# Delta-rule stage of a two-block network: the filler projections leave PSUM by a ScalarE copy, and VectorE applies their row factor from SBUF

## The chip, the cores and the metric

The kernel runs on one core of a Trainium2 chip. The metric is device time in microseconds, lower is better: the median of three runs is 1378.98 us (1376.60 to 1381.67). The profile is of one further execution of 1386.14 us.

## What is computed

The input has 256 tokens of width 1024. A first block (token mixer and channel mixer) and a second block follow each other. The change lies in the middle of the second block, in its gated delta rule and multiscale pool:

```python
h = _rmsnorm(x, norm_mix_w[l])
proj = h @ w_in[l]
qkv = proj[..., :3 * DN_WIDTH]
z = proj[..., 3 * DN_WIDTH:4 * DN_WIDTH]
...
p = proj[..., 4 * DN_WIDTH + 2 * DN_HEADS:]
qkv = jax.nn.silu(_causal_conv(qkv, conv_w[l])).astype(jnp.float32)
q = _l2norm(qkv[..., :DN_WIDTH].reshape(b, s, DN_HEADS, DN_HEAD_DIM))
k = _l2norm(qkv[..., DN_WIDTH:2 * DN_WIDTH].reshape(b, s, DN_HEADS, DN_HEAD_DIM))
...
o = _chunk_gated_delta_rule(q, k, v, g, beta)
o = _rmsnorm(o, dn_norm_w[l]) * jax.nn.silu(z...)
pool_out = _multiscale_pool(p, w_pool[l], pool_scale[l]).astype(x.dtype)
x = x + jnp.concatenate([o, pool_out], axis=-1) @ w_out[l]
```

A lookup over 16384 experts (PEER) and a last norm follow. The delta rule holds a triangular inverse per head; the kernel builds it in blocks of 16 and then doubles the block size three times.

## The kernel before

Activations lie transposed: 128 channels on the partitions, 256 tokens along the free axis. A projection of 128 output channels is eight steps over the 1024 inputs, and each step is three matmuls (lines 375 to 377), because inputs and weights are split into a high and a low fp32r part. So a projection is 24 matmuls into one PSUM tile `pb`, of which there are three (`bufs=3`).

Weights come through a stream (class `Stream`): a DMA brings a `raw` tile of 512 KB (four of them), ScalarE rounds it to `whi` (line 218) and VectorE subtracts to get `wlo` (line 231). In this stage five such pairs exist, and a new DMA starts when a `wlo` has been made.

The rmsnorm's factor of each token, `rs` (tile `rbs`), is applied to a projection's result after the matmuls. So each projection ends with a step that reads PSUM, multiplies by `rs` and writes SBUF. That step also gives the PSUM tile back.

The stage has two strands. The main strand (`main`) is the delta rule: decay factors `dec` and the mask `N`, the products of k with k (line 1532), sums of squares and their reciprocal root (lines 1377, 425 to 448), the 16-block inverse as a long run of small VectorE instructions (lines 636 and 639, tiles `itmp` and `zd`), then its transpose `TT` and three doublings (lines 1581, 1591, 1586). The other strand (`filler`) holds the 16 projections for q, v, the pool p and z, in this order, and then the pool's half of the output projection. `weave` draws them against each other by weights written in the program, and a scheduler then fixes the order of each engine's instructions; each engine runs its own list strictly in that order.

A filler projection (`fproj`) runs 24 matmuls and hands its PSUM tile on; what follows it (multiply, convolution taps at line 1306, tanh, last product at line 1295, or the pool's windows at line 1424) is put into the list `post`, and one entry is taken from it at every matmul step of the following projections:

```python
for kt in range(KD):
    self.proj_step(ps, w, xs, kt)
    pop()
    yield 0.33
```

For q and v the first entry is `first` of `conv_ops` (line 1302, into tile `ct`), for the pool line 1434 (into `pp`), for z line 1415 (into `zt`). All are one VectorE `tensor_tensor` of 128 x 256 from PSUM. The four k projections come from before the stage and use `conv_ops` with a tile given from outside (`vn`).

Of the kernel before, what the change touches and what calls it, by code (L numbers as in the profile page):

```python
# [9 lines left out]
F32 = mybir.dt.float32  # L10
# [6 lines left out]
ALU = mybir.AluOpType  # L17
PSUM = bass.MemoryType.PSUM
P = 128
T = 256  # L20
# [276 lines left out]
class Builder:  # L297
# [949 lines left out]
    def delta(self, xs, pre, rs):  # L1247
        tc, nc, i, S = self.tc, self.nc, self.i, self.S
        x = self.x
        V, A, G = nc.vector, nc.scalar, nc.gpsimd  # L1250
        mm = nc.tensor.matmul
        b4 = lambda ps: ps.rearrange("p (c s) -> p c s", c=4)
        with tc.tile_pool(name="del", bufs=1) as dp:
# [7 lines left out]
            pp = t4("pp")  # L1261
# [7 lines left out]
            post = []  # L1269
# [7 lines left out]
            def fproj(eng):  # L1277
                ps = (self.pb if "f" in st else self.pa)()[:, 0:T]
                st["f"] = 1
                w = S.get()  # L1280
# [4 lines that stand above are left out]
                S.split(eng)  # L1285
                return ps

            def silu_ops(dst, src, th=None):
                d = {}

                def tanh():
                    d["th"] = dp.tile([P, T], F32, name="th", tag="th", bufs=4) if th is None else th
                    A.activation(d["th"], src, AF.Tanh, scale=0.5)

                return tanh, lambda: V.scalar_tensor_tensor(dst, d["th"], 1.0, src, ALU.add, ALU.mult)

            def conv_ops(dst, ps, ch, ct=None, th=None):
                d = {}

                def first():  # L1300
                    d["t"] = dp.tile([P, T], F32, name="ct", tag="ct", bufs=4) if ct is None else ct
                    V.tensor_tensor(d["t"], ps, rs, ALU.mult)  # L1302
                    A.activation(dst, d["t"], AF.Copy, scale=self.par("conv2", 36 + ch))

                def tap(s):
                    V.scalar_tensor_tensor(dst[:, s:T], d["t"][:, 0:T - s], self.par("conv2", (3 - s) * 12 + ch),
                                           dst[:, s:T], ALU.mult, ALU.add)

                tanh, last = silu_ops(dst, dst, th)
                return [first, lambda: tap(1), lambda: tap(2), lambda: (tap(3), tanh()), last]  # L1310

            sp = dp.tile([P, 2, 8], F32, name="sp")
            s24 = lambda n: dp.tile([P, 2, 4], F32, name=n)
# [44 lines left out]
            def head():  # L1358
                V.tensor_scalar(dnh, self.par("dn"), 0.5, None, ALU.mult)
                go = gate_ops()  # L1360
                next(go)
                vt = vn.rearrange("p (h a) t -> p h (a t)", h=4)
                kc = [conv_ops(k[:, h, :], ps, 4 + h, vt[:, h, :], o[:, h, :]) for h, ps in enumerate(pre)]
                for n in range(5):
                    for ops in kc:
                        ops[n]()
                        if n:
                            next(go, None)
                        yield YL[0]
                for _ in go:  # L1370
                    yield 0.2
# [29 lines left out]
            def conv_part(dst, base, name):  # L1401
                for h in range(4):
                    ps = yield from fproj(DS[h % 2])
                    c = conv_ops(dst[:, h, :], ps, base + h)
                    post.extend([c[0], None, c[1], c[2], c[3], None, c[4], None])
                post.append(lambda: st.update({name: 1}))

            def z_part():
                for h in range(4):
                    ps = yield from fproj(DZ[h % 2])  # L1410
                    t = dp.tile([P, T], F32, name="zt", tag="zt", bufs=2)
                    tanh, last = silu_ops(z[:, h, :], t)

                    def first(t=t, ps=ps, tanh=tanh):
                        V.tensor_tensor(t, ps, rs, ALU.mult)
                        tanh()

                    post.extend([first, None, None, last, None, None, None, None])

            def windows(g):  # L1420
                cur, s = pp[:, g, :], 1
                while s < win[g]:
                    n = dp.tile([P, T], F32, name="pw", tag="pw", bufs=3)
                    G.tensor_tensor(n[:, s:T], cur[:, s:T], cur[:, 0:T - s], ALU.add)
                    A.copy(n[:, 0:s], cur[:, 0:s])
                    cur, s = n, 2 * s
                st["p", g] = cur

            def pool_part():
                for g in range(4):  # L1430
                    ps = yield from fproj(DS[g % 2])

                    def first(g=g, ps=ps):
                        V.tensor_tensor(pp[:, g, :], ps, rs, ALU.mult)
                        windows(g)

                    def second(g=g):
                        cur = st["p", g]
                        V.tensor_tensor(cur[:, 0:16], cur[:, 0:16], self.con("rc", g * 16, g * 16 + 16), ALU.mult)
                        V.scalar_tensor_tensor(cur, cur, 1.0 / win[g], pp[:, g, :], ALU.mult, ALU.subtract)  # L1440

                    post.extend([first] + [None] * 6 + [second, lambda g=g: pool_mm(g)])
                post.append(lambda: st.update({"p": 1}))

            def filler():
                for part in ORD:
                    if part == "q":
                        yield from conv_part(q, 0, "q")
                    if part == "v":
                        yield from conv_part(v, 8, "v")  # L1450
                    if part == "z":
                        yield from z_part()
                    if part == "p":
                        yield from pool_part()
                while post:
                    pop()
                    yield 0.33
                while "acc" not in st:
                    yield 0.5
                for g in range(4):  # L1460
                    if g == NAR:
                        S.narrow()
                    yield from self.gout_step(st["acc"], (yah[:, g, :], yal[:, g, :]), g == 0, False)
                    S.split({"G": G, "V": V, "B": both}[GO[g]])

            def pool_mm(g):
                ps = self.pb()[:, 0:T]
                mm(ps, wpl[:, g * P:(g + 1) * P], st["p", g], start=True, stop=True)
                po = dp.tile([P, T], F32, name="po", tag="po", bufs=2)
                A.activation(po, ps, AF.Copy, scale=self.par("pool_scale", g))  # L1470
                self.split(yah[:, g, :], yal[:, g, :], po, G)
# [200 lines left out]
            for h in range(4):  # L1672
                ps = self.pb()
# [368 lines left out]
```

## Time and profile before

| | |
|---|---|
| median of three runs | 1378.98 us |
| profiled execution | 1386.14 us, of which the span is 1384.1 us |
| TensorE (PE) busy | 1341.7 us, 97% |
| VectorE (DVE) busy | 990.2 us, 72% |
| ScalarE (ACT) busy | 681.2 us, 49% |
| GpSimd (POOL) busy | 236.4 us, 17% |
| mean granted TensorE clock | 0.976 of full speed |

Times inside the profile are microseconds from the start of the span. PE is TensorE's matmuls, PEld its weight loads, SP the engine that issues DMAs. The delta-rule stage reaches from about 438 to 556 us. Names are the program's tiles without buffer numbers, L1302 is line 1302. A matmul's own duration overlaps with the next one's, so the pace is read from the distance between starts. [...]

### The profile page before, as it was taken

How to read it: one execution, taken by the hardware profiler on the slowest of the kernel's cores; microseconds unless marked ns; L12 is line 12 of the kernel's file. 1: busy time of each engine (PE TensorE's matmuls, PEld its weight loads, DVE VectorE, ACT ScalarE, POOL GpSimd, SP SyncE). 2: the span in 40 equal slices, each digit the busy share in tenths (PEclk: the TensorE clock that was granted, in tenths of full speed). 3: DMA queues.
4: the chain of work that ended last, by engine and by line, in shares of the span. 5: the costliest groups of instructions: out<-in, count | busy, mean ns of one | idle time of the engine just before them, and what ended most of it. 6: DMA issues, size and time to landing. Idle time of an engine off the chain costs nothing.

```text
span 1384.1 us, 26933 instructions
## 1 busy us (share of the span) xinstructions
PE 1341.7 (97%) x10572; PEld 1255.3 (91%) x10572; DVE 990.2 (72%) x2104; ACT 681.2 (49%) x1256; POOL 236.4 (17%) x218
## 2 busy tenths in 40 slices
PE   7989998999999799999999999999999999999998
PEld 6878997999998799999999999999998888888886
DVE  7863677888877886799995777888865555545554
ACT  3521355655565533465554554444444554554454
POOL 5610333010005240200000000000012222222221
PEclk9888998999999899999999999999999999999999
DMA  6140352566553132445555454544555555555553
GB/s 227 55 112 33 107 168 93 191 203 212 185 175 104 50 107 90 143 149 179 179 183 175 158 165 157 167 157 164 164 186 199 191 193 195 197 187 195 197 193 111
DMA packets 64334, 217.89 MB, mean 157 GB/s; under 512 B 10272, under 2 KB 11248, under 8 KB 64080
## 3 DMA queue, kind: packets, MB, share of 16 engines
q1 hardware_dynamic: 59376, 212.76, 46.5%
q0 software_dynamic: 992, 2.72, 0.7%
q8 instruction: 83, 1.36, 0.4%
q10 hardware_dynamic: 3840, 0.70, 0.4%
q14 instruction: 43, 0.35, 0.1%
HBM read 214.70 MB, written 1.44 MB: 156 GB/s over the span
## 4 chain that ended last, share of the span: by engine, by line
PE 87%; DVE 6%; ACT 2%; POOL 2%; DMA 1%; issue 1%; ACTq 0%; SPq 0%; POOLq 0%
PE pa L1950 25%; PE pb L375 15%; PE pb L376 15%; PE pb L377 15%; PE pa L375 3%; PE pa L376 3%; PE pa L377 3%; PE pc L1904 1%; PE pb L1904 1%; PE pa L1064 1%; PE pa L1581 1%; ACT whi L218 1%; DVE wlo L231 0%; PE pb L1838 0%; PE pc L463 0%
## 5 line engine op out<-in xcount | busy, mean ns | idle before, releaser
L218 ACT ACTIVATE whi<-raw 128x1024 fp32r<-128x1024 f32 x396 | 418.3, 1058 | 518.7 <-PE pb L376 260.4
L231 DVE TENSOR_TENSOR wlo<-raw,whi 128x1024 fp32r<-128x1024 f32 x382 | 467.1, 1223 | 249.8 <-ACT whi L218 248.7
L375 PE MATMUL pb<-xnh,whi 128*128 128x256 f32 x1024 | 294.3, 288 | 0.0
L376 PE MATMUL pb<-xnl,whi 128*128 128x256 f32 x1024 | 289.7, 283 | 0.0
L377 PE MATMUL pb<-xnh,wlo 128*128 128x256 f32 x1024 | 289.0, 283 | 0.0
L1950 PE MATMUL pa<-whi,up 128*128 128x512 f32 x1024 | 274.5, 389 | 0.0
L1950 PEld LDWEIGHTS pa<-whi,up 128*128 128x128 f32 x1024 | 192.2, 188 | 39.8
L376 PEld LDWEIGHTS pb<-xnl,whi 128*128 128x128 f32 x1024 | 196.1, 191 | 0.0
L375 PEld LDWEIGHTS pb<-xnh,whi 128*128 128x128 f32 x1024 | 195.9, 191 | 0.0
L377 PEld LDWEIGHTS pb<-xnh,wlo 128*128 128x128 f32 x1024 | 195.7, 191 | 0.0
L375 PE MATMUL pb<-xh,whi 128*128 128x256 f32 x648 | 187.8, 290 | 4.2 <-DVE ct L1302 4.2
L376 PE MATMUL pb<-xl,whi 128*128 128x256 f32 x648 | 185.6, 286 | 0.3
L377 PE MATMUL pb<-xh,wlo 128*128 128x256 f32 x648 | 185.4, 286 | 0.0
L1950 PE MATMUL pa<-wlo,up 128*128 128x512 f32 x512 | 158.3, 389 | 0.0
L503 POOL TENSOR_TENSOR up<-hb,up 128x256 fp32r<-128x256 f32 x32 | 45.9, 1434 | 553.3 <-ACT up L502 553.3
L375 PEld LDWEIGHTS pb<-xh,whi 128*128 128x128 f32 x648 | 123.7, 191 | 5.5 <-DVE ct L1302 4.4
L376 PEld LDWEIGHTS pb<-xl,whi 128*128 128x128 f32 x648 | 123.8, 191 | 1.5 <-DVE xl L569 0.9
L377 PEld LDWEIGHTS pb<-xh,wlo 128*128 128x128 f32 x648 | 123.7, 191 | 0.6
L1950 PEld LDWEIGHTS pa<-wlo,up 128*128 128x128 f32 x512 | 96.1, 188 | 20.0
L503 POOL TENSOR_TENSOR up<-scr,up 128x256 fp32r<-128x256 f32 x32 | 47.1, 1472 | 127.0 <-ACT up L502 127.0
L231 POOL TENSOR_TENSOR wlo<-raw,whi 128x1024 fp32r<-128x1024 f32 x19 | 46.5, 2453 | 43.3 <-ACT whi L218 34.4
L376 PE MATMUL pa<-al,whi 128*128 128x256 f32 x176 | 49.0, 281 | 0.0
(546 smaller groups left out, 2214.9 us busy)
## 6 DMA issues: line engine op xcount, KB each, us to landing
raw<-down SPq DMA_DIRECT2D x128, 512.0 KB, 3.3
raw<-up SPq DMA_DIRECT2D x128, 512.0 KB, 3.3
raw<-w_in SPq DMA_DIRECT2D x46, 512.0 KB, 3.4
raw<-w_up SPq DMA_DIRECT2D x44, 512.0 KB, 3.5
raw<-w_down SPq DMA_DIRECT2D x22, 512.0 KB, 3.4
raw<-w_out SPq DMA_DIRECT2D x16, 512.0 KB, 3.3
raw<-w_query SPq DMA_DIRECT2D x16, 512.0 KB, 3.4
x<-xT SPq DMA_DIRECT2D x4, 256.0 KB, 5.6
```

The source lines that it names most:

```text
L218: nc.scalar.activation(hi, self.raw[self.nh], AF.Copy)
L231: e.tensor_tensor(lo[:, a:z], raw[:, a:z], hi[:, a:z], ALU.subtract)
L375: mm(ps, w[0], x[0], start=start, stop=False, **k)
L376: mm(ps, w[0], x[1], start=False, stop=False, **k)
L377: mm(ps, w[1], x[0], start=False, stop=stop, **k)
L503: (eng or self.nc.vector).tensor_tensor(lo, src, hi.bitcast(F32), ALU.subtract)
L1064: mm(out[h, q], lh[h, 8 * hf + q, 0:64], self.halves(rh[h, 8 * hf + q, :], l, odd), start=True, stop=True)
L1581: mm(out[:, h], lh[:, tb * 4 + h, :], self.halves(rh[:, tb * 4 + h, :], l, odd), start=True, stop=True)
L1904: mm(ps[:, n, :], e1[:, q, :, r], eg[m][:, q, :, r], start=(m == 0), stop=(m == 1))
L1950: mm(acc[tb * 2 + hf], a[:, ts], b[:, hf * 512:hf * 512 + 512], start=False, stop=(e == 127 and lo == 1), skip_group_check=True)
```

## The change

Each of the 16 filler projections now leaves PSUM by a plain ScalarE copy, and VectorE multiplies by `rs` in place in SBUF. The copy is the first entry of `post`, the multiply the second. The k projections keep the old form.

```diff
             def conv_ops(dst, ps, ch, ct=None, th=None):
                 d = {}
 
+                def lift():
+                    d["t"] = dp.tile([P, T], F32, name="ct", tag="ct", bufs=4) if ct is None else ct
+                    A.copy(d["t"], ps)
+
                 def first():
-                    d["t"] = dp.tile([P, T], F32, name="ct", tag="ct", bufs=4) if ct is None else ct
-                    V.tensor_tensor(d["t"], ps, rs, ALU.mult)
+                    if "t" in d:
+                        V.tensor_tensor(d["t"], d["t"], rs, ALU.mult)
+                    else:
+                        d["t"] = ct
+                        V.tensor_tensor(ct, ps, rs, ALU.mult)
                     A.activation(dst, d["t"], AF.Copy, scale=self.par("conv2", 36 + ch))
...
-                return [first, lambda: tap(1), lambda: tap(2), lambda: (tap(3), tanh()), last]
+                return [first, lambda: tap(1), lambda: tap(2), lambda: (tap(3), tanh()), last, lift]
...
-                    post.extend([c[0], None, c[1], c[2], c[3], None, c[4], None])
+                    post.extend([c[5], c[0], c[1], c[2], c[3], None, c[4], None])
...
-                    def first(t=t, ps=ps, tanh=tanh):
-                        V.tensor_tensor(t, ps, rs, ALU.mult)
+                    def first(t=t, tanh=tanh):
+                        V.tensor_tensor(t, t, rs, ALU.mult)
                         tanh()
-                    post.extend([first, None, None, last, None, None, None, None])
+                    post.extend([lambda t=t, ps=ps: A.copy(t, ps), first, None, last, None, None, None, None])
...
-                    def first(g=g, ps=ps):
-                        V.tensor_tensor(pp[:, g, :], ps, rs, ALU.mult)
+                    def first(g=g):
+                        V.tensor_tensor(pp[:, g, :], pp[:, g, :], rs, ALU.mult)
                         windows(g)
...
-                    post.extend([first] + [None] * 6 + [second, lambda g=g: pool_mm(g)])
+                    post.extend([lambda g=g, ps=ps: A.copy(pp[:, g, :], ps), first] + [None] * 5 + [second, lambda g=g: pool_mm(g)])
```

The scheduler orders the instructions anew around this; the lists of all engines differ inside this stage alone. Three places show it. Lines behind the edit are numbered up to 7 higher in the changed kernel, and buffer numbers differ by a few. A line of "..." stands for rows left out, mostly the other matmuls of a projection.

TensorE before, around the main strand's way from k to the 16-block inverse: `pb_5930`, `pb_6104`, `pb_6200` and `pb_6240` are filler projections, `pa_5745` is k with k, `pc_5755` the sums of k's squares, `pa_5826` and `pa_5858` feed the 16-block inverse.

```order
L377 MATMUL pb_5930<-xh_5233,wlo_5570 128x256
L1532 MATMUL pa_5745<-k_5456 128x128 x4
...
L1377 MATMUL pc_5755<-ones_89,sq_5756 128x1 x2
...
L620 MATMUL pa_5826<-itmp_5776,con_del_3354 128x128
L629 MATMUL pa_5858<-dg_5774,sel_3362 128x128 x4
...
L375 MATMUL pb_6104<-xh_5233,whi_5639 128x256
...
L375 MATMUL pb_6200<-xh_5233,whi_5689 128x256
...
L375 MATMUL pb_6240<-xh_5233,whi_5838 128x256
```

Between k with k and the inverse no projection stands here.

The same place of TensorE in the changed kernel, where `pb_5934`, `pb_6109`, `pb_6206`, `pb_6247` are the same four projections, `pb_6288` and `pb_6401` the next two:

```order
L377 MATMUL pb_5934<-xh_5233,wlo_5570 128x256
L375 MATMUL pb_6109<-xh_5233,whi_5640 128x256
...
L1539 MATMUL pa_5748<-k_5456 128x128 x4
...
L375 MATMUL pb_6206<-xh_5233,whi_5691 128x256
...
L1384 MATMUL pc_5758<-ones_89,sq_5759 128x1 x2
...
L375 MATMUL pb_6288<-xh_5233,whi_5928 128x256
...
L620 MATMUL pa_5829<-itmp_5779,con_del_3354 128x128
L629 MATMUL pa_5862<-dg_5777,sel_3362 128x128 x4
...
L377 MATMUL pb_6247<-xh_5233,wlo_5843 128x256
...
L377 MATMUL pb_6288<-xh_5233,wlo_5930 128x256
...
L375 MATMUL pb_6401<-xh_5233,whi_6103 128x256
...
L377 MATMUL pb_6401<-xh_5233,wlo_6105 128x256
```

One whole projection has moved ahead of k with k, and 23 of the 24 matmuls of the next ahead of the sums. Behind the inverse's first products stand `pb_6247` and `pb_6288`, where `pb_6104` and `pb_6200` stood.

VectorE right behind the 16-block inverse, before (`ct_6111`, `ct_6207`, `ct_6247` are the multiplies that read PSUM):

```order
L639 TENSOR_REDUCE zd_5775<-itmp_5776 128x4 x2
L1306 SCALAR_TENSOR_TENSOR v_5458<-ct_5937,params_85,v_5458 128x254
L231 TENSOR_TENSOR wlo_6100<-raw_5643,whi_6098 128x1024
L1302 TENSOR_TENSOR ct_6111<-pb_5930,rbs_5431 128x256
L231 TENSOR_TENSOR wlo_6196<-raw_5693,whi_6194 128x1024
L646 TENSOR_SCALAR Z_5484<-zd_5775,con_del_3354 128x8x16 x4
L1302 TENSOR_TENSOR ct_6207<-pb_6104,rbs_5431 128x256
L1306 SCALAR_TENSOR_TENSOR v_5458<-ct_5937,params_85,v_5458 128x253
L1302 TENSOR_TENSOR ct_6247<-pb_6200,rbs_5431 128x256
```

And the same place of VectorE in the changed kernel:

```order
L639 TENSOR_REDUCE zd_5778<-itmp_5779 128x4 x2
L1313 SCALAR_TENSOR_TENSOR v_5458<-ct_5941,params_85,v_5458 128x254
L231 TENSOR_TENSOR wlo_6105<-raw_5644,whi_6103 128x1024
L1306 TENSOR_TENSOR ct_6116<-ct_6116,rbs_5431 128x256
L231 TENSOR_TENSOR wlo_6202<-raw_5695,whi_6200 128x1024
L646 TENSOR_SCALAR Z_5484<-zd_5778,con_del_3354 128x8x16 x4
L1306 TENSOR_TENSOR ct_6213<-ct_6213,rbs_5431 128x256
L1313 SCALAR_TENSOR_TENSOR v_5458<-ct_5941,params_85,v_5458 128x253
L231 TENSOR_TENSOR wlo_6243<-raw_5845,whi_6241 128x1024
L1306 TENSOR_TENSOR ct_6254<-ct_6254,rbs_5431 128x256
L231 TENSOR_TENSOR wlo_6284<-raw_5932,whi_6282 128x1024
L1441 TENSOR_TENSOR pp_5459<-pp_5459,rbs_5431 128x256 x2
```

The instructions are the same ones in nearly the same order, with SBUF in the place of PSUM as the source.

ScalarE in the changed kernel around the squares of k (`sq`), with three of the new copies:

```order
L1302 COPY ct_5941<-pb_5847 128x256
L1527 ACTIVATE dec_5478<-dec_5478 128x512
...
L218 ACTIVATE whi_6103<-raw_5644 128x1024
L1302 COPY ct_6116<-pb_5934 128x256
L517 ACTIVATE sq_5759<-k_5456 128x256
...
L218 ACTIVATE whi_6200<-raw_5695 128x1024
L1302 COPY ct_6213<-pb_6109 128x256
```

Before, the multiplies that freed `pb_5930` and its successor `pb_6104` stood on VectorE behind the 16-block inverse; the copies that free them now stand on ScalarE beside the squares of k, ahead of the inverse.

## Rows read from the trace of the kernel before

**Rows 1.** Windows of the stage: busy us (instructions) of each engine, then granted clock.
```profile
457.70:475.40 17.70, 13.33 (x88) 12.71 (x87) 14.62 (x67) 7.94 (x20) 4.91 (x5) 0.71 0.18 60
475.40:486.00 10.60, 6.45 (x55) 6.25 (x53) 10.59 (x55) 6.47 (x16) 3.02 (x3) 0.99 0.01 3
486.00:505.10 19.10, 19.05 (x151) 19.01 (x152) 18.08 (x45) 7.24 (x16) 4.51 (x3) 0.92 0.43 138
505.10:525.40 20.30, 20.30 (x175) 20.14 (x174) 11.93 (x25) 7.47 (x19) 8.49 (x11) 1.00 0.24 79
...
555.00:560.00 5.00, 5.00 (x35) 4.99 (x35) 1.28 (x5) 1.36 (x2) 0.00 (x0) 0.75 0.06 22
```
**Rows 2.** Waits of TensorE, 438 to 505 us: total us, times, longest.
```profile
PE pb L375 <- DVE ct L1302: 4.2, 1, 4.2
PE pc L1377 <- DVE rv L425: 1.4, 1, 1.4
PE pa L620 <- DVE itmp L618: 1.3, 1, 1.3
PE pc L1377 <- ACT sq L517: 1.0, 1, 1.0
```
**Rows 3.** Timeline of TensorE: start us, us, instruction, count [idle before, releaser].
```profile
457.72 1.95 PE L1532 MATMUL pa<-k 128*128 128x128 f32 x16
...
460.66 2.48 PE L1377 MATMUL pc<-ones,sq 128*128 128x1 f32 x16 [0.99 <-ACT sq L517]
...
467.64 0.80 PE L620 MATMUL pa<-itmp,con_del 128*128 128x128 f32 x2 [1.27 <-DVE itmp L618]
...
478.09 0.28 PE L375 MATMUL pb<-xh,whi 128*128 128x256 f32 x1
...
478.45 0.28 PE L375 MATMUL pb<-xh,whi 128*128 128x256 f32 x1
...
486.05 0.58 PE L375 MATMUL pb<-xh,whi 128*128 128x256 f32 x1 [4.19 <-DVE ct L1302]
...
504.94 0.67 PE L1581 MATMUL pa<-TT,N 128*128 128x64 f32 x5
```
**Rows 4.** Timeline of VectorE, same columns.
```profile
458.88 0.69 DVE L1536 TENSOR_TENSOR N<-pa,N 128x512 f32<-128x512 f32 x1 [1.72 <-PE pa L1532]
...
464.17 0.22 DVE L425 TENSOR_SCALAR rv<-pc 128x4 f32<-128x4 f32 x2
...
467.30 0.29 DVE L618 TENSOR_TENSOR itmp<-byk,con_del 128x128 f32<-128x128 f32 x1
...
484.44 1.22 DVE L231 TENSOR_TENSOR wlo<-raw,whi 128x1024 fp32r<-128x1024 f32 x1
...
485.57 0.42 DVE L1302 TENSOR_TENSOR ct<-pb,rbs 128x256 f32<-128x256 f32 x1
...
488.16 0.48 DVE L1306 SCALAR_TENSOR_TENSOR v<-ct,params,v 128x253 f32<-128x253 f32 x1
...
488.55 0.42 DVE L1302 TENSOR_TENSOR ct<-pb,rbs 128x256 f32<-128x256 f32 x1
...
498.03 1.16 DVE L1295 SCALAR_TENSOR_TENSOR v<-th,v 128x256 f32<-128x256 f32 x2
...
502.27 0.41 DVE L1586 TENSOR_TENSOR TT<-TT,pa 128x256 f32<-128x256 f32 x1
```
**Rows 5.** Groups by line: busy us, mean ns, idle before (438 to 560; whole span).
```profile
L1302 DVE TENSOR_TENSOR ct<-pb,rbs 128x256 f32<-128x256 f32 x7 | 2.9, 419 | 0.0
...
L1847 ACT COPY scr<-pb 128x256 f32<-128x256 f32 x16 | 5.7, 354 | 0.0
```
**Rows 6.** Tile sq on VectorE, both inputs in SBUF: ns min/median/max.
```profile
L536 DVE TENSOR_TENSOR sq<-sq x10: 411/424/426, 202.3 to 428.5; 128x256 f32<-128x256 f32 x10
L803 DVE TENSOR_TENSOR sq<-sq x4: 411/412/829, 8.3 to 17.3; 128x256 f32<-128x256 f32 x4
```
**Rows 7.** Timeline of TensorE at the stage's end.
```profile
553.02 0.54 PE L455 MATMUL pb<-con_base,yo 128*128 128x128 f32 x3 [2.63 <-DVE yo L448]
```

## The prediction

> **What bounds the kernel now.** I read the windows of the stage first. TensorE does nearly all the work of this kernel, so what the change can be worth is TensorE's idle time in the stage, and what its clock loses behind it. From 505.1 to 525.4 it is busy for the whole 20.30 us at full clock [rows 1], so nothing is to be had there. The losses lie earlier: 17.70 - 13.33 = 4.4 us idle at a mean clock of 0.71 from 457.7 on, 10.60 - 6.45 = 4.2 us idle up to 486.0, then a clock of 0.92 over 19.1 us, which costs 0.08 x 19.1 = 1.5 us. VectorE is the other thing to see in these rows: 10.59 of 10.60 us, then 18.08 of 19.10 us. It is full exactly where TensorE waits.
>
> The waits name what ended each gap [rows 2]: 4.2 us for the multiply `ct` of line 1302, and 1.0, 1.4 and 1.3 us on the main strand's way into the 16-block inverse. In the timeline of TensorE [rows 3] the 4.19 us lie before 486.05, when filler projections have no free PSUM tile. In VectorE's timeline [rows 4] the multiply that ended them starts at 485.57, behind a weight subtraction at 484.44, and that stands behind the whole inverse. So PSUM is held by VectorE's list, and the change goes at this.
>
> **The change part by part.** Removed: 16 VectorE multiplies out of PSUM, 0.42 us each [rows 5]. Added: 16 ScalarE copies out of PSUM; the same shape at line 1847 takes 0.354 us [rows 5], 5.7 us in all. ScalarE has 17.70 - 7.94 and 10.60 - 6.47 us free in the two windows of the loss [rows 1]; I cost the copies at nothing. Should one come late, TensorE waits for it as it waited for `ct`, and no more.
>
> Added too: 16 VectorE multiplies from SBUF. The nearest row with both inputs in SBUF is line 536, 0.424 us in the middle of ten, against 0.419 us for the multiply from PSUM [rows 5, 6]. So I take the exchange as zero and VectorE is not relieved at all. [...]
>
> Moved: TensorE's list. With tiles free earlier, 24 filler matmuls go ahead of k with k, and 23 more ahead of the sums of squares. Three matmuls take 0.36 us (478.09 to 478.45 [rows 3]), so a projection is 2.87 us. Now follow the main strand. k with k started at 457.72 and takes 1.95 us; it will start 2.87 us later, at 460.6, and end at 462.5. Then 23 matmuls, 2.75 us, then the sums: 2.48 us before, partly at the lower clock, about 2.0 us if the clock holds. They end at 467.3. The reciprocal root (`rv`, 464.17 before [rows 4]) then starts at 467.4. It is 3.1 us from that start to the start of `itmp` at 467.30; two small steps of the same chain stood behind `rv` and will be done before it (some 0.46 us, the same kind as the 0.22 to 0.29 us rows there). So line 620, at 467.64 before [rows 3], moves to about 470.4: **+2.8 us for the main strand**. The gaps of 1.0 and 1.4 us on TensorE are filled with useful work, but VectorE, which has to do the inverse, stands idle for it (it already idled 1.72 us before 458.88 [rows 4]).
>
> From line 620 on VectorE is full until the first doubling of the inverse has updated `TT`, which began at 502.27 [rows 4]. I take this as the meeting point, since the matmul that reads `TT` starts the last gap-free stretch. Behind the inverse the new list brings one weight subtraction and one pool multiply forward (484.44 to 485.57 is 1.13 us, a multiply steps by 0.33 us: together 1.5) and puts two taps (0.39 us each, 488.16 to 488.55), three last products of v (1.16 us for two at 498.03, so some 1.1 to 1.7 us) and two pool products (about 0.7 us) behind the meeting point: some 2.6 us. Net **-1.1 us**. `TT` is then ready 2.8 - 1.1 = 1.7 us later, at 502.27 + 0.41 + 1.7 = 504.4.
>
> Before, TensorE took up that `TT` only at 504.94 [rows 3], 2.3 us after it was ready, since two projections more stood in front. In the changed list they are gone by then, so it goes on at once: **-2.3 us**. But it has one pool matmul (a product of two records, some 0.25 us) and three filler matmuls (0.36 us) still to do: **+0.6 us**.
>
> What of the 4.2 us before 486? The PSUM tile is now free, but the new list puts `pb_6401` there, whose third matmul needs `wlo_6105`. That subtraction is where `wlo_6100` was, right behind the inverse, 484.44 + 1.13 + 2.8 = 488.4. TensorE gets there after line 629, the small products and two projections, about 484, and waits some 4 us again. So the wait changes its name. It costs nothing further, since `TT` is later than what follows it.
>
> A new gap appears just before the meeting point. After 488.4 TensorE has 22 filler matmuls and the main strand's products, without fillers between them, and is done around 502; then it waits for `TT`, some 2.4 us. Does the clock fall? [...] Bounds: nothing, or the 1.5 us after the 4.19 us gap. I take **+1.25 us**, from the row nearest in length.
>
> Sum: 2.8 - 1.1 - 2.3 + 0.6 + 1.25 = **+1.2 us**. Behind the meeting point TensorE has the same work in nearly the same order, without a gap before and none to be won. The tail (the 2.63 us wait for the last root) keeps its order. Against the profiled execution (1386.14 us, span 1384.1) that is 1387.4 us; it stood 7.2 us over the median of 1378.98, so for the median I say **1380.2 us**. A measurement of this kernel can tell some 0.5% from no change, that is 6.9 us: below 1372.1 or above 1385.9.
>
> **The rivals.** *The main strand is not held up.* If the squares or k come late anyway, or the fillers fit in TensorE's gaps, the 2.8 us and the clock's 1.25 us go: -1.1 - 2.3 + 0.6 = -2.8 us, 1376.2. For it: 3.7 us of gaps were there [rows 2]. Against it: k with k was gated by k itself, ready at once, and a whole projection now stands in front.
>
> *PSUM is the whole story.* VectorE's list turns out not to be last, and the two projections that run ahead are all gained: 2 x 2.87 = 5.7 us, 1373.2. Against it: VectorE had 0.01 us free in 10.60 [rows 1].
>
> *GpSimd and VectorE get in each other's way*, the rival on the slow side. A multiply with both inputs in SBUF has once taken 0.829 us instead of 0.412 at line 803 [rows 6], +0.42 us. Eleven of the new multiplies (eight for q and v, three for the pool) stand ahead of the meeting point, and GpSimd is busy 4.91, 3.02 and 4.51 us in the three windows there [rows 1]. If all are hit: 11 x 0.42 = 4.6 us on the full engine, 1.2 + 4.6 = +5.8, 1384.8 us; it decides as soon as more than three are hit, being then above my sum's own error. Against it: line 536 shows 0.426 at most in ten. [...]
>
> *The copies come no earlier than the multiplies did*, since ScalarE's list puts them behind weight roundings that wait. Then the order changes and the release does not: 4.2 us of wait stay and TensorE gains nothing, 1379 to 1383. Against it: the copy that frees `pb_5930`'s counterpart stands ahead of k's squares, which ScalarE began to deliver at 460.66 [rows 3].
>
> **How the numbers follow.** Forecast, 1377 to 1383 with the errors of a chain of some ten terms: 0.65. Main strand not held up: 0.13. PSUM the whole story: 0.06, half of it beyond 0.5%. Contention: 0.11, a third of it beyond. Copies late: 0.05. So faster by over 0.5% has 0.05, slower 0.08 with something for what I did not see, and no difference 0.87. The range runs from the second rival's 1373 to the contention case with one us of scatter, 1386.
>
> **What would show it.** Right: the wait of TensorE for `ct` gone and one of some 4 us for `wlo` in its place; line 620 near 470; VectorE full from there to about 504; a gap before the reader of `TT`; the windows behind 505 unchanged. Wrong: line 620 still at 467 to 468 (first rival); a stage that ends 5 us earlier (second); multiplies in place well over 0.45 us and longer GpSimd rows beside them (third); waits of TensorE for a ScalarE copy (fourth). A change in any stage before 438 or after 560 would be outside all of this.

## The result, and the profile after

The changed kernel takes **1387.11 us** (median of 9 runs, 1383.98 to 1392.34), the kernel before beside it 1379.91 us (9 runs, 1376.60 to 1381.94). The ratio is **1.0057, interval 1.0042 to 1.0073**: slower by some 7 us. Forecast were 1380.2 us and a range up to 1386.0, so the time lies outside.

The profiled execution after took 1383.98 us (span 1382.1), the lowest of its nine. The one before was long for its kernel (1386.14 us) and reached this stage 7.79 us later, so the spans can't be compared. The two stages can, from one instruction to another. I take the transposes of the gate's input (TensorE, line 1328 before, 1335 after) as the start, and the first matmul that reads `yo` as the end. Before, then after:

```profile
437.19 0.28 PE L1328 MATMUL pa<-con_base,bt 8*128 8x8 f32 x2
...
549.89 0.49 PE L455 MATMUL pb<-con_base,yo 128*128 128x128 f32 x3
```
```profile
429.40 0.28 PE L1335 MATMUL pa<-con_base,bt 8*128 8x8 f32 x2
...
547.82 0.49 PE L455 MATMUL pb<-con_base,yo 128*128 128x128 f32 x3
```

Behind that end both executions go on for the same 834.2 to 834.3 us. From start to end it is 112.70 us before and 118.42 after: **the stage is 5.72 us longer**, just under the lower end of what the interval of the ratio allows (5.8 to 10.1 us).

The windows of [rows 1] go by the time in the span, and at the same time the changed kernel is 7.79 us further into the stage. So I cut both kernels at the same instructions instead: line 620, the transposes of `Z` (line 1570 before, 1577 after), the transposes of v (1622 and 1629), and the reader of `yo` (columns as in [rows 1], then the share of the DMA engines and GB/s). Before, then after:

```profile
467.64:490.40 22.76, 17.86 (x123) 17.36 (x124) 22.07 (x90) 11.68 (x27) 3.13 (x3) 0.83 0.28 89
490.40:513.42 23.02, 23.02 (x200) 22.91 (x199) 18.72 (x45) 9.43 (x23) 11.42 (x12) 1.00 0.31 102
513.42:549.89 36.47, 36.47 (x312) 36.36 (x312) 21.82 (x53) 11.65 (x19) 2.04 (x3) 1.00 0.21 70
```
```profile
466.24:488.24 22.00, 17.21 (x119) 16.82 (x120) 21.10 (x89) 12.13 (x28) 3.14 (x3) 0.84 0.29 82
488.24:511.22 22.98, 19.68 (x151) 18.75 (x150) 19.30 (x45) 8.29 (x23) 6.16 (x8) 0.93 0.32 106
511.22:547.82 36.60, 36.60 (x313) 36.49 (x313) 22.52 (x55) 13.79 (x26) 3.99 (x6) 1.00 0.20 73
```

VectorE is still nearly full in the first stretch, and TensorE has idle time in the second (3.30 us) where it had none. The third is gap-free at full clock, as before. Together they are 0.67 us shorter than before, so the loss lies ahead of line 620. Here are TensorE's waits in the changed kernel, 430 to 512 us, against [rows 2]:

```profile
PE pb L377 <- DVE wlo L231: 4.1, 1, 4.1
PE pa L1516 <- POOL gt L1362: 2.8, 1, 2.8
PE pa L620 <- DVE itmp L618: 1.7, 1, 1.7
PE pa L1588 <- DVE TT L1593: 1.7, 1, 1.7
```

The wait for `ct` is gone, and one of 4.1 us for `wlo` stands in its place, as forecast. New is the second row: **TensorE waits 2.8 us for GpSimd**, for `gt`, the log of the decay. My prediction does not mention that tile. It ends a chain of some twenty tiny GpSimd operations (128 x 8) at the head of the stage, which I call the gate chain, lines 1334 to 1355 before and 1341 to 1362 after (the diff adds seven lines).

Here is that chain in GpSimd's timeline of the changed kernel (start us, us, instruction), with what VectorE did beside its two longest operations:

```profile
429.97 0.20 POOL L1341 TENSOR_TENSOR z<-sp,ab 128x8 f32<-128x8 f32 x1 [3.84 <-DVE sp L1337]
430.64 1.18 POOL L1347 TENSOR_SCALAR beta<-beta 128x8 f32<-128x8 f32 x1 [0.47 <-ACT e L1343]
...
434.70 1.02 POOL L1355 TENSOR_TENSOR l<-l,w 128x8 f32<-128x8 f32 x1
...
437.33 1.81 POOL L1356 TENSOR_SCALAR l<-l 128x8 f32<-128x8 f32 x1
...
440.72 1.82 POOL L1360 TENSOR_SCALAR l<-l 128x8 f32<-128x8 f32 x1
...
442.98 0.31 POOL L1362 TENSOR_TENSOR gt<-l,ea 128x8 f32<-128x8 f32 x1
```
```profile
437.50 1.22 DVE L231 TENSOR_TENSOR wlo<-raw,whi 128x1024 fp32r<-128x1024 f32 x1
438.64 0.41 DVE L1306 TENSOR_TENSOR ct<-ct,rbs 128x256 f32<-128x256 f32 x1
...
440.88 1.22 DVE L231 TENSOR_TENSOR wlo<-raw,whi 128x1024 fp32r<-128x1024 f32 x1
442.02 0.41 DVE L1306 TENSOR_TENSOR ct<-ct,rbs 128x256 f32<-128x256 f32 x1
```

An operation of this size takes 0.20 us where VectorE does nothing beside it (the first row). The one at 437.33 takes 1.81: it ends at 439.14, just after the weight split `wlo` *and* the new in-place multiply behind it (439.05). In the kernel before, GpSimd was held up three times, by one `wlo` each (the splits end at 439.50, 443.26 and 447.49, the three long operations 0.05 to 0.11 us later):

```profile
438.43 1.18 POOL L1340 TENSOR_SCALAR beta<-beta 128x8 f32<-128x8 f32 x1 [0.46 <-ACT e L1336]
...
442.30 1.02 POOL L1348 TENSOR_TENSOR l<-l,w 128x8 f32<-128x8 f32 x1
...
446.13 1.41 POOL L1350 TENSOR_TENSOR l<-l,e 128x8 f32<-128x8 f32 x1
...
448.42 0.31 POOL L1355 TENSOR_TENSOR gt<-l,ea 128x8 f32<-128x8 f32 x1
```

From the start of `z` (437.76 before, 429.97 after) to the end of `gt` the chain takes 10.97 us before and **13.32 after**. Two things are new: the multiply reads both inputs from SBUF, and VectorE's order has moved, so that a fourth `wlo` falls into the chain.

What the late `gt` does to TensorE, first before, then after:

```profile
448.78 0.39 PE L1509 MATMUL pa<-gt,con_del 128*128 128x8 f32 x2 [0.49 <-POOL gt L1355]
449.03 2.03 PE L1514 MATMUL pa<-con_del,gt 128*128 128x128 f32 x16
```
```profile
443.34 0.60 PE L1516 MATMUL pa<-gt,con_del 128*128 128x8 f32 x2 [2.83 <-POOL gt L1362]
443.79 3.35 PE L1521 MATMUL pa<-con_del,gt 128*128 128x128 f32 x16
...
456.68 1.95 PE L1539 MATMUL pa<-k 128*128 128x128 f32 x16
...
466.24 0.49 PE L620 MATMUL pa<-itmp,con_del 128*128 128x128 f32 x2 [1.69 <-DVE itmp L618]
...
500.40 1.27 PE L1588 MATMUL pa<-TT,N 128*128 128x64 f32 x8 [1.66 <-DVE TT L1593]
```

The same sixteen matmuls take 3.35 us instead of 2.03: after the gap TensorE runs below its full clock, at 0.50 of it from 443.34 to 446.34 and at 1.00 again from 447.34 on. Windows of four kernels, from the transposes of the gate's input to the reader of `gt`, and from there to k with k (columns as above). The kernel before:

```profile
437.19:448.78 11.59, 11.10 (x92) 10.87 (x91) 10.84 (x28) 7.71 (x15) 8.66 (x22) 1.00 0.61 212
448.78:457.72 8.94, 8.94 (x76) 8.94 (x76) 7.46 (x20) 6.54 (x18) 0.45 (x1) 1.00 0.31 112
```

The changed kernel:

```profile
429.40:443.34 13.94, 11.11 (x93) 10.88 (x92) 13.11 (x32) 8.91 (x19) 11.00 (x22) 0.99 0.61 210
443.34:456.68 13.34, 13.34 (x99) 13.34 (x100) 6.89 (x17) 8.54 (x24) 2.12 (x2) 0.88 0.11 37
```

The changed kernel with the row factor read from PSUM (the first experiment):

```profile
429.79:442.88 13.09, 11.11 (x93) 10.88 (x92) 12.38 (x31) 8.45 (x19) 10.14 (x22) 1.00 0.65 223
442.88:454.70 11.82, 11.82 (x100) 11.82 (x101) 7.52 (x19) 9.03 (x25) 2.13 (x2) 1.00 0.14 46
```

The changed kernel with q heads 0 to 2 in the old form (the fourth):

```profile
430.62:442.20 11.58, 11.10 (x93) 10.87 (x92) 10.83 (x27) 7.70 (x15) 8.65 (x22) 1.00 0.62 207
442.20:453.53 11.33, 11.33 (x95) 11.33 (x96) 8.02 (x21) 8.93 (x25) 2.49 (x2) 1.00 0.25 89
```

So of the 5.72 us, 2.35 are the wait for `gt` (13.94 - 11.59) and 4.40 lie up to k with k (13.34 - 8.94). Of the 4.40, the projection that now stands there, 24 more matmuls, makes about 2.9 (100 records in 11.82 us against 76 in 8.94, both at full clock), and the mean clock of 0.88 makes the other 1.5 (13.34 against 11.82 for practically the same matmuls). The rest of the stage gives 1.0 us back.

### The profile page after: what moved, and what is told of

Its sections match the earlier page's. It is cut to its first block, busy times and chain, and to the rows that moved or that the text cites. A ratio compares the mean times of both kernels' runs of the same rounds, so it can differ in the third digit from the quotient of the medians.

```text
span 1382.1 us, 26943 instructions
## 1 busy us (share of the span) xinstructions
PE 1338.2 (97%) x10572; PEld 1253.8 (91%) x10572; DVE 991.9 (72%) x2104; ACT 685.4 (50%) x1272; POOL 236.1 (17%) x218
## 4 chain that ended last, share of the span: by engine, by line
PE 88%; DVE 7%; ACT 2%; POOL 2%; DMA 1%; issue 1%; SPq 0%; ACTq 0%; DVEq 0%; POOLq 0%
PE pa L1957 25%; PE pb L375 15%; PE pb L376 15%; PE pb L377 15%; PE pa L375 3%; PE pa L376 3%; PE pa L377 3%; PE pc L1911 1%; PE pb L1911 1%; PE pa L1064 1%; DVE wlo L231 1%; ACT whi L218 1%; PE pa L1588 1%; PE pc L463 1%; PE pb L1845 0%
```

## The experiments

Theory 1: the new multiplies stand in the way of the gate chain. Theory 2: TensorE's new order costs it. Theory 3: the copies do. Ratios are against the kernel before in the same series; its median was 1379.94, 1379.88 and 1379.76 us in the three.

**One operand back to PSUM.** The PSUM source of the row factor's copy is kept, and q heads 0 to 2 multiply by that:

```diff
-self.nc.scalar.copy(rs, ps[:, 0:T])
+self.nc.scalar.copy(rs, ps[:, 0:T]); self.rsp = ps[:, 0:T]
...
-V.tensor_tensor(d["t"], d["t"], rs, ALU.mult)
+V.tensor_tensor(d["t"], d["t"], self.rsp if ch < 3 else rs, ALU.mult)
```

> The changed kernel with one operand changed in three instructions: the multiplies of q heads 0 to 2 read the row factor from its PSUM tile instead of its SBUF copy, so that each has one SBUF input as before. The order on every engine is that of the changed kernel. Theory 1 (the two-SBUF-input multiplies stand in the way of GpSimd's small operations of the gate chain): the chain from z8 to the end of gt goes from 13.3 us back to 11.0 +- 0.4, gt's first reader on TensorE comes 11.6 us after the transposes of bt instead of 13.9, the products k x k come about 4 us earlier, and the time is 1383 (1381.5 to 1384.5), what is left over before being the order. Theory 2 (the filler projections that now stand ahead of the k x k products and of the sums of squares cost it): nothing is changed in that, 1387 (1386 to 1388.5), whatever the gate chain does. Theory 3 (the sixteen copies on ScalarE cost it): 1387 too, and the gate chain stays at 13.3.

Measured 1382.82 us, ratio 1.0021 (1.0004 to 1.0037); chain 12.46 us. GpSimd's two long operations, the multiply beside the first, and TensorE behind the chain:

```profile
437.71 1.47 POOL L1356 TENSOR_SCALAR l<-l 128x8 f32<-128x8 f32 x1
...
441.13 1.41 POOL L1361 TENSOR_TENSOR l<-l,z 128x8 f32<-128x8 f32 x1
```
```profile
439.02 0.41 DVE L1306 TENSOR_TENSOR ct<-ct,pc 128x256 f32<-128x256 f32 x1
```
```profile
442.88 0.39 PE L1516 MATMUL pa<-gt,con_del 128*128 128x8 f32 x2 [1.98 <-POOL gt L1362]
443.12 2.03 PE L1521 MATMUL pa<-con_del,gt 128*128 128x128 f32 x16
```

With the order of every engine unchanged, the time falls by 4.3 us and lies where theory 1 put it; theories 2 and 3 said 1387. In the profiled executions the stage takes 116.22 us, 2.20 less than the changed kernel's. The operand is worth 0.86 us of the chain (13.32 to 12.46). The other 1.49 us of the chain's growth stay: four `wlo` still fall into it, in VectorE's new order. I had expected 11.0, which was wrong, and theory 1 as I put it has no place for that part.

This pair of runs has the same instructions and one input moved: beside the multiply with both inputs in SBUF GpSimd's operation took 1.81 us and ended just after the multiply, beside the one with a PSUM input it took 1.47 us and ended at 439.18, just after the split ahead (439.10).

**Copies kept, multiply from PSUM** for q and v, over the copy:

```diff
-V.tensor_tensor(d["t"], d["t"], rs, ALU.mult)
+V.tensor_tensor(d["t"], ps, rs, ALU.mult)
```

> The changed kernel with all ScalarE copies of the twelve q and v... heads kept in place for q and v, but the multiply of q and v reading the projection from PSUM again, over the copy. On TensorE the work up to the inverse then stands as in the kernel before: 57 filler matmuls between the gate products and the k x k products, and the twelve sums in one piece. Theory 1: the gate chain takes 11.0 +- 0.4 us; time as before, 1380 (1378.5 to 1382). Theory 2: the order is the old one, so as before too, 1380 (1378.5 to 1382). Theory 3 (the copies): 1386 to 1388, since all copies are there.

(The edit concerns the eight heads of q and v; "twelve" is a slip.) Measured 1381.36 us, ratio 1.0012 (1.0000 to 1.0024); chain 12.44 us, not 11.0, for the reason just given. Theory 3 falls: all sixteen copies are on ScalarE's list, and the time is 1.4 us above that of the kernel before.

**Only q lifted.** z and pool multiply from PSUM as before, and for v:

```diff
-post.extend([c[5], c[0], c[1], c[2], c[3], None, c[4], None])
+post.extend([c[5], c[0], c[1], c[2], c[3], None, c[4], None] if name == "q"
+            else [c[0], None, c[1], c[2], c[3], None, c[4], None])
```

> Only the four q projections are copied out and multiplied from SBUF; v, z and the pooling projections are as before. On TensorE 81 filler matmuls stand ahead of the k x k products as in the changed kernel, but the twelve sums are in one piece as before. Theory 1: the three multiplies beside the gate chain are those of q, so the chain is at 13.3 +- 0.4 us and most of the loss is there: 1385.5 (1384 to 1387.5). Theory 2: the half of the order's cost that lies ahead of the k x k products remains, 1383.5 (1382 to 1385). Theory 3: four copies of sixteen, 1381.5 (1380 to 1383).

Measured 1386.07 us, ratio 1.0053 (1.0033 to 1.0072); chain 13.30 us. Four of the sixteen edits, those beside the gate chain, bring nearly the whole loss. That is theory 1's 1385.5; theory 2 said 1383.5 and theory 3 1381.5.

**q heads 0 to 2 old, the other thirteen lifted.**

```diff
-post.extend([c[5], c[0], c[1], c[2], c[3], None, c[4], None])
+post.extend([c[0], None, c[1], c[2], c[3], None, c[4], None] if name == "q" and h < 3
+            else [c[5], c[0], c[1], c[2], c[3], None, c[4], None])
```

> The changed kernel with q heads 0 to 2 in the old form (no copy, the multiply reads PSUM); the other thirteen projections are lifted. On TensorE 77 filler matmuls stand ahead of the k x k products and 21 ahead of the first sums, nearly the changed kernel's order. Theory 1: gate chain 11.0 +- 0.4 us, time 1383 (1381.5 to 1384.5), as the kernel with the operand changed. Theory 2: 1386 to 1388. Theory 3 (thirteen copies of sixteen): 1385 to 1387.

Measured **1380.72 us**, ratio 1.0001 (0.9989 to 1.0013), under theory 1's 1381.5. The chain takes 10.95 us with three blocks, as before, and TensorE waits 0.48 us for `gt`. TensorE's order is nearly the changed one (the second window above: 95 records, 11.33 us), and thirteen copies are there. So these two together cost some 2 us at most: the interval ends at 1.8 us, and the profiled stage takes 114.75 us, 2.05 more than before. VectorE's order beside the chain is the old one again here, with three splits in it, so this run alone doesn't part the operand from that order.

**The form of the multiply.** In the changed kernel's timeline the convolution's taps (`scalar_tensor_tensor`, two SBUF tensors) lengthen GpSimd's operations only to 0.27 to 0.34 us, once to 0.46, and once, at 440.02 with a last product of k beside it too, to 0.61. Is it the form?

```diff
-V.tensor_tensor(d["t"], d["t"], rs, ALU.mult)
+V.scalar_tensor_tensor(d["t"], d["t"], 1.0, rs, ALU.mult, ALU.mult)
```

> The changed kernel with one instruction form changed: the in-place multiplies of q and v, still with both inputs in SBUF, are issued as scalar_tensor_tensor (times 1.0, times the row factor), the form of the convolution's taps, beside which GpSimd's small operations took only 0.23 to 0.35 us. The order on every engine is that of the changed kernel. Theory 1a (it is the form tensor_tensor with two SBUF inputs that holds GpSimd up): the chain is at 12.4 +- 0.3 us as in the kernel with the operand changed, the time at 1382.8 (1381.5 to 1384.5). Theory 1b (any VectorE operation with two SBUF inputs holds GpSimd up, whatever its form): the chain stays at 13.3 +- 0.3 and the time at 1387 (1385.5 to 1388.5).

Measured 1386.03 us, ratio 1.0040 (1.0024 to 1.0057); chain 13.30 us, with the same two long operations beside the new form:

```profile
444.59 1.81 POOL L1356 TENSOR_SCALAR l<-l 128x8 f32<-128x8 f32 x1
```
```profile
445.90 0.41 DVE L1306 SCALAR_TENSOR_TENSOR ct<-ct,rbs 128x256 f32<-128x256 f32 x1
```

Theory 1a falls. The same with the weight splits (the subtractions that make `wlo`), on the kernel before and, with the multiplies, on the changed one:

```diff
-e.tensor_tensor(lo[:, a:z], raw[:, a:z], hi[:, a:z], ALU.subtract)
+(e.scalar_tensor_tensor(lo[:, a:z], raw[:, a:z], 1.0, hi[:, a:z], ALU.mult, ALU.subtract)
+ if e is self.b.nc.vector else e.tensor_tensor(lo[:, a:z], raw[:, a:z], hi[:, a:z], ALU.subtract))
```

> The kernel before, with VectorE's splits of the weights (wlo, line 231, in the whole kernel) issued as scalar_tensor_tensor (raw times 1.0, minus whi) in place of tensor_tensor; orders as in the kernel before. Theory 1a: the three long operations of the gate chain (1.18, 1.02 and 1.41 us) go to about 0.3 each, the chain from 11.0 to 8.3 +- 0.5 us; gt's reader on TensorE then waits for nothing, each wlo costs about 0.06 us more on VectorE, and the time is 1378.5 (1374 to 1380.5). Theory 1b: chain 11.0 +- 0.3, time 1380 to 1382.

Measured 1380.40 us, ratio 1.0006 (0.9994 to 1.0018), chain 10.97: no change, as 1b said.

> The changed kernel with both: the in-place multiplies of q and v and VectorE's splits of the weights as scalar_tensor_tensor; orders as in the changed kernel. Theory 1a: nothing holds GpSimd up any more, the chain goes from 13.3 to 8.5 +- 0.5 us, what remains against the kernel before is the order alone, so 1380.5 (1377 to 1382), about 2 us above the kernel before with the same splits. Theory 1b: 13.3 us and 1387 to 1389. Theory 2 (the order alone costs it): 1386 to 1388 whatever the chain does.

Measured 1385.86 us, ratio 1.0039 (1.0024 to 1.0053), chain 13.31: 1b again, for a time 1 us lower than it said.

**The gate chain on VectorE**, as here for all its GpSimd operations in `gate_ops`:

```diff
-G.tensor_tensor(z8, sp[:, :, 4:8], ab[:, 1:2, :].to_broadcast([P, 2, 4]), ALU.add)
+V.tensor_tensor(z8, sp[:, :, 4:8], ab[:, 1:2, :].to_broadcast([P, 2, 4]), ALU.add)
```

> The changed kernel with the gate chain's small operations moved from GpSimd to VectorE, so that nothing of VectorE can hold the chain up by contention; the planned orders shift with it (171 filler matmuls and eight of the twelve sums now stand ahead of gt's reader). Theory 1: without the contention the loss is gone up to the cost of some twenty operations of about 0.15 us on VectorE: 1381 (1378 to 1385). Theory 2 says nothing of this order; with more fillers ahead of the k x k products it would be slower than the changed kernel, over 1388.

Measured 1385.27 us, ratio 1.0034 (1.0018 to 1.0049), just past theory 1's bound. Theory 1 had put it at 1381, theory 2 over 1388, so both numbers missed. It decides nothing: the order moved too far. TensorE's longest wait is now 7.6 us for `dg`, further down the main strand.

**The taps' exact form**, the scalar 1.0 read from an SBUF column:

```diff
-V.tensor_tensor(d["t"], d["t"], rs, ALU.mult)
+V.scalar_tensor_tensor(d["t"], d["t"], self.ones[:, 0:1], rs, ALU.mult, ALU.mult)
```

> The changed kernel with the in-place multiplies of q and v in the taps' exact form: scalar_tensor_tensor with its scalar (1.0) read from an SBUF column, both tensors in SBUF, 256 columns. TensorE's and GpSimd's orders are those of the changed kernel. Theory 3a (the taps spare GpSimd because their scalar is read from SBUF): the chain is at 12.4 +- 0.3 us, the time at 1383 (1381.5 to 1384.5). Theory 3b (they spare it because their operands are shifted and of odd length): the chain stays at 13.3 +- 0.3, the time at 1386 to 1387.

Measured 1383.34 us, ratio 1.0036 (1.0022 to 1.0050); chain 12.69 us, and the operation is at 1.47 us as with the PSUM operand:

```profile
437.84 1.47 POOL L1356 TENSOR_SCALAR l<-l 128x8 f32<-128x8 f32 x1
```
```profile
439.14 0.48 DVE L1306 SCALAR_TENSOR_TENSOR ct<-ct,ones,rbs 128x256 f32<-128x256 f32 x1
```

So this multiply has two SBUF tensors and yet lets GpSimd in behind `wlo` (at 439.31, where the split ended at 439.22), with VectorE's order beside the chain that of the changed kernel. It costs VectorE 0.48 us instead of 0.41.

**Odd length**, 255 columns and one:

```diff
-V.tensor_tensor(d["t"], d["t"], rs, ALU.mult)
+V.tensor_tensor(d["t"][:, 0:255], d["t"][:, 0:255], rs[:, 0:255], ALU.mult)
+V.tensor_tensor(d["t"][:, 255:256], d["t"][:, 255:256], rs[:, 255:256], ALU.mult)
```

> The changed kernel with each in-place multiply of q and v cut in two tensor_tensor instructions, of 255 columns and of one. Theory 3b in the narrow sense that the odd length decides: chain 12.4 +- 0.3 us, time 1383 to 1385 with eight small instructions more on VectorE. Theory 3a, or the shift of the operands rather than their length: chain 13.3 +- 0.4, time 1386 to 1388.

Measured 1386.60 us, ratio 1.0054 (1.0041 to 1.0067), chain 13.40: the length is not it.

**Splits in the taps' form** on the kernel before, then with the multiplies on the changed one. The edit is that of the three-operand splits with `self.b.ones[:, 0:1]` for 1.0.

> The kernel before with VectorE's splits of the weights in the taps' form (scalar 1.0 from an SBUF column). Theory 3a: the chain goes from 11.0 to 8.3 +- 0.6 us; each split costs some 0.06 us more on VectorE and takes nothing from GpSimd; 1378.5 (1375 to 1381). Theory 3b: 11.0 +- 0.3 us and 1380 to 1383.

Measured **1378.54 us**, ratio 0.9987 (0.9978 to 0.9997): it beats both kernels, the one before by 0.13% and the changed one by some 0.6% (by the medians). But not for theory 3a's reason. The chain takes 10.77 us, not 8.3, and a split still holds GpSimd to its end:

```profile
433.95 1.20 POOL L1349 TENSOR_SCALAR l<-l 128x8 f32<-128x8 f32 x1
```
```profile
433.77 1.28 DVE L231 SCALAR_TENSOR_TENSOR wlo<-raw,ones,whi 128x1024 fp32r<-128x1024 f32 x1
```

The chain fits theory 3b, the time theory 3a. The stage is no shorter (113.00 us against 112.70). The gain lies elsewhere, the planned order having moved in the whole kernel, and I did not follow it. The scalar from SBUF does not make an operation harmless in general: in the multiply, GpSimd gets in between it and the split ahead, while the three splits held it for 1.23, 1.20 and 1.15 us, each time to just after its own end.

> The changed kernel with both in the taps' form, the in-place multiplies of q and v and VectorE's splits of the weights. Theory 3a: chain 8.5 +- 0.6 us, what is left against the kernel before is the order, 1380.5 (1377.5 to 1383). Theory 3b: 13.3 us, 1386 to 1389.

Measured 1380.51 us, ratio 1.0003 (0.9991 to 1.0015), on the number expected but again not for its reason: the chain takes 10.84 us, with three blocks of one split each (1.24, 1.19 and 1.14 us). This is the whole change, all copies included, at the time of the kernel before. Against the kernel that has only these splits (1378.54 us) it is still 2.0 us longer, as much as the order and the copies cost above.

All kernels whose chain is on GpSimd, by its length; the stage is that of the profiled execution, from the transposes of the gate's input to the reader of `yo` ("SBUF scalar" is the taps' form):

| chain, us | kernels | medians, us | stage, us |
|---|---|---|---|
| 10.8 to 11.0 | before; q 0 to 2 old; splits three-operand; splits SBUF scalar; both SBUF scalar | 1379.9, 1380.7, 1380.4, 1378.5, 1380.5 | 112.7, 114.8, 112.7, 113.0, 115.2 |
| 12.4 to 12.7 | factor from PSUM; copy but PSUM; multiply SBUF scalar | 1382.8, 1381.4, 1383.3 | 116.2, 115.5, 116.8 |
| 13.3 to 13.4 | changed; only q; three-operand; both three-operand; odd | 1387.1, 1386.1, 1386.0, 1385.9, 1386.6 | 118.4, 118.2, 118.6, 118.5, 119.3 |

Neither the medians nor the stages of the three groups overlap, while copies, order and instruction forms differ within them. (The intervals of the ratios do overlap between the second and the third: the multiply with the SBUF scalar has 1.0022 to 1.0050.) Against the kernel before, the last group's chain is 2.4 us longer and its time 6 to 7. Of that surplus 1.5 us are visible in the changed kernel as the clock, and some 2 us are TensorE's order and the copies.

The stages also split the 5.72 us into three steps: 2.05 us for the change without q heads 0 to 2 (114.75), 1.47 more with them in VectorE's new order but the operand in PSUM (116.22), and 2.20 more for the operand in SBUF (118.42). The last step changes one operand and no order. The middle one is about the chain's 1.49 us, which the trace puts down to the fourth split; no run changes that order alone.

## Why the prediction was wrong

*The step that failed* is "Added too: 16 VectorE multiplies from SBUF ... So I take the exchange as zero." It looked at the multiply's own duration alone, and that was right: 420 ns after, against 419 in [rows 5]. The copies took 387 ns where 354 was taken. The groups of the changed kernel, 425 to 560 us (busy us, mean ns, idle before):

```profile
L1306 DVE TENSOR_TENSOR ct<-ct,rbs 128x256 f32<-128x256 f32 x8 | 3.4, 420 | 0.0
L1302 ACT COPY ct<-pb 128x256 f32<-128x256 f32 x7 | 2.7, 387 | 0.0
```

What it left out is who else is held while the operation runs. The run with the operand changed shows 0.86 us of chain from that; the rest, 1.49 us, is put down to VectorE's new order, in which a fourth split runs before the chain is through. "Moved: TensorE's list" followed TensorE's order alone, and VectorE's only from line 620 on. The sum had no term for the gate chain at all. It began at k with k, and [rows 2] began at 438 us, with the wait for `gt`, 0.49 us then, below its smallest row.

*The contention rival* had the right mechanism and the wrong engine. It priced "11 x 0.42 = 4.6 us on the full engine", VectorE, and so reached 1384.8 us. No multiply was lengthened (411 to 427 ns, all sixteen). The loser in the gate chain was GpSimd, and what made it dear was that TensorE already waited 0.49 us for its result, so that nothing covered a delay. GpSimd was held beside two multiplies, those of q heads 1 and 2, so "it decides as soon as more than three are hit" was wrong too. VectorE can lose as well: beside GpSimd's window sums (128 x 255 and 128 x 254) the split at 490.88 us took 1.63 us instead of 1.22, and the taps at 490.12 and 492.43 took 0.84 and 0.82 instead of 0.47. These are instructions that the rival did not price.

*Main strand, +2.8 us at line 620*: measured +6.4 from the start of the stage. Without the wait for `gt` (2.35) and the clock behind it (1.5) that leaves 2.5, so the term for the order held. The projection ahead of k with k cost 2.9 us in a window at full clock (11.82 against 8.94), forecast 2.87. From k with k to line 620 it was 9.56 us against 9.92: the sums' fillers cost nothing.

The wait for `wlo` (TensorE) and the update of `TT` (VectorE) in the changed kernel:

```profile
484.00 0.49 PE L377 MATMUL pb<-xh,wlo 128*128 128x256 f32 x1 [4.08 <-DVE wlo L231]
```
```profile
499.94 0.41 DVE L1593 TENSOR_TENSOR TT<-TT,pa 128x256 f32<-128x256 f32 x1
```

*VectorE's work moved behind `TT`, -1.1*: from line 620 to the update of `TT` 33.70 us (499.94 - 466.24) against 34.63, so -0.9. *Slack before its reader, -2.3*: the reader started 2.67 us after the update's start before, 0.46 after, so -2.2. *Wait for `wlo`, some 4 us*: 4.08, at 484.00. *Gap before the reader of `TT`, 2.4 us*: 1.66. *Clock and work left, +1.85*: from the reader to the end of the stage it is 47.42 us (547.82 - 500.40) against 44.95, so +2.5. The 1.25 us of clock in this term were an estimate from one place of the kernel before (0.75 in the last line of [rows 1], behind the 2.63 us of [rows 7]); behind the 1.66 us here the clock was 0.66 over 5.00 us, as an estimate 0.34 x 5.00 = 1.7 us. Together with the 2.35 and the 1.5 these make 2.35 + 1.5 + 2.5 - 0.9 - 2.2 + 2.5 = 5.75 us, the stage's 5.72.

So six terms of the forecast stood within 0.8 us, and one that was not in it cost 3.9 us in the trace. The kernel that takes only q heads 0 to 2 out of the change came to 1380.72 us, where the forecast for the whole change was 1380.2; it leaves three copies out and keeps VectorE's old order beside the chain, so this is no exact test of the other terms.

The median lies a further 1.5 us over what the profiled stage shows (7.2 against 5.7). The profiled execution was the lowest of its nine, and what the others lost, and where, no profile of this kernel tells, so that part stays open.

*Copies late*: in the list of TensorE's waits between 430 and 512 us none is for the copy of a projection. *PSUM the whole story* and *main strand not held up* fell with the rows above.

## What to carry to other kernels

Moving an operand from PSUM to SBUF is not only a question of the instruction's own time: look at what GpSimd is doing beside it (here an operation of 1.47 us became one of 1.81), and who waits for that. A chain of tiny GpSimd operations that ends on TensorE's path is a place where a delay can be paid more than once: here 2.35 us of it became 2.35 us of wait and 1.5 us of lower clock behind it. Before a change that lets VectorE run ahead, list the waits that are short now, not only the long ones: the one that grew was the one that had been 0.49 us.

## What was not expected of the hardware

The hold carried over from one VectorE operation to the next. In the changed kernel GpSimd's operation at 437.33 came free after the split *and* the multiply (1.81 us), but the one at 434.70 came free between a split and a multiply (1.02 us), with the same pair of instructions beside it. What sets the two apart stayed open. The trace shows two differences: the operation that came free earlier started 0.26 us after the split and is a `tensor_tensor`, while the two that were held through both (437.33 and 440.72) started 0.16 to 0.17 us ahead of the split and are `tensor_scalar`. In all five kernels of the last group the `tensor_tensor` took 1.02 us and the two `tensor_scalar` 1.81 to 1.82, so these runs can't tell which of the two counts.

A multiply with two SBUF tensors lets GpSimd in when its scalar comes from SBUF too (chain 12.69 us, against 13.30 with the scalar in the instruction). Theory 1b, that any two SBUF inputs hold GpSimd up, does not cover this, and why the two differ was not shown.

A gap of 1.98 us ahead of the reader of `gt` was followed by full clock in one kernel (2.03 us for the sixteen matmuls, factor from PSUM) and by less in another (3.48 us, copy but PSUM), and one of 2.22 us by full clock again (2.03 us, multiply with the SBUF scalar). After 2.83 us in the changed kernel and in the one with only q lifted it was lower (3.35 and 3.36 us). The length of the gap alone does not tell what the clock does.
